# Splitting queries, keys and values ahead of attention and computing all gates in pairs, in a one-core hybrid encoder layer

## The chip, the core and the metric

The kernel is one program on one core of a Trainium2 chip. A core has a matrix engine (PE, with its weight loads shown apart as PEld), a vector engine (DVE), an activation engine (ACT), a general engine (POOL) and a queue engine that issues transfers (SP). They run side by side and wait for each other through semaphores. On-chip memory is SBUF (128 partitions); matmul results land in PSUM, which has eight banks here; DRAM is off the chip, reached by DMA. The metric is the device time of one execution in microseconds, as the median of several runs.

## What is computed

One encoder layer over 1024 tokens of width 1024, in float32. Cut to what matters for the change:

```python
proj = x @ w_in                       # q_a, k_a, v_a, f_a | q_b, f_b, i_b, g_b | gate_a, gate_b
y_a = fox_attention(q_a, k_a, v_a, log_sigmoid(f_a + b_f))   # 8 heads of 64, causal softmax
                                      # logit[t,s] = q_t.k_s/8 + F[t] - F[s]
y_b = hgrn2_chunkwise(silu(q_b), 1 - f, i_b, log(f))         # 4 heads of 128, gated recurrence
merged = sigmoid(gate_a) * (y_a @ w_pa) + sigmoid(gate_b) * (y_b @ w_pb)
x = layer_norm(ALPHA * x + merged @ w_o)
x = layer_norm(ALPHA * x + (silu(g) * u) @ w_ff_out)         # u, g = x @ w_ff_in
```

`gate_a` and `gate_b` are each 1024 columns wide: 16 blocks of 128 columns together, called gates 0 to 15 below.

## The kernel before

**Precision.** Every float32 operand of a big product is split into a high and a low part (`split`: ACT casts the high part, DVE subtracts it from the source), and a product is three matmuls (`mm3`): high by high, high by low, low by high. Each is 128 x 128 weights against 512 columns.

**Strassen pairs.** Many products are done as 2 x 2 block products with 7 sub-products in place of 8 (names p1 to p7). For two gates as a pair that is 7 x 4 x 3 = 84 matmuls, where two plain gates take 2 x 2 x 8 x 3 = 96. The sums that this needs are made by DVE.

**Stages, in order of time.** The values of both branches (`vx`, `vy`); queries and keys by `qk_strassen`, one call for each of four pairs of heads; attention, eight heads; HGRN, four heads; the rest of the gates; the two branch projections (`pps`); the output projection (`o`); the first and the second half of the feed-forward net (`fa`, `fb`, `fc`; then `p`).

**Attention before.** `qk_first` runs `qk_strassen` for the pairs 1, 2, 3, 0. For pairs 1 to 3, `put` stores the float32 result in DRAM (`qk_d`, 12 stores of 128 KB a pair). For pair 0, `qk_heads` splits it into the operands at once. After each pair of heads `qk_load` fetches the next pair (eight loads of 256 KB into `qkr`) and splits it with eight ACT and eight DVE instructions. A head's operands are `q2` (high and low query stacked on the partitions), `k2` (high key twice) and `kl` (low key twice). They sit in the buffers "qk" (six of them; two `q2` and two `kl` a pair) and "kb" (four; two `k2` a pair). Values are kept on the chip as `va` (buffer "v"), and each head splits its part into `vhl` with one ACT and one DVE instruction. The last four blocks of probabilities of a head are up to 1024 wide and take all four buffers "pf", so the wide blocks of a head wait for those of the head before.

**What fills PE's gaps.** Attention and HGRN are chains across PE, DVE, ACT and POOL. Between their steps PE does work that hangs on nothing there: in attention four plain gates (`gate`, results `gps`; as many as the constant `PLAIN` says), then the even gate of the later pairs (`gate_part`, results `ge`: products p1 and p2 of the pair, 24 matmuls), and the projections of the HGRN heads (`hgrn_project`, results `bps`, 144 matmuls a head). Gates 4 to 7 are two pairs interleaved (`pairs`), and gates 8 to 15 four more pairs in a loop, five products (60 matmuls) each after their `gate_part`; both write `gs`.

**Order of the work.** The body of the kernel does not issue instructions. It records them in a `Plan`; `schedule` then places them in time by a table of costs, engine by engine, with the buffers' waiting lines, and `improve` repeats this with ranks counted back from the end (`latest`), `ROUNDS` times, with random slack from the seventh on, and keeps the order whose planned end is earliest. `issue` emits that order; each engine then runs its own list strictly in order. So any edit can change the whole order. All instructions are issued at line 381, which is why all profile rows carry L381. `plan.behind` makes the calls recorded while it is set wait for a given earlier call.

Of the kernel before, what the change touches and what calls it, by code (L numbers as in the profile page):

```python
# [24 lines left out]
FF = 2816  # L25
CHUNKS = [[(0, n)] if n <= NB else [(0, n - w), (n - w, w)] for n, w in
          ((128, 0), (256, 0), (384, 0), (512, 0), (640, 256), (768, 256), (896, 384), (1024, 512))]
PLAIN = 4
MERGE = {"g": "s"}
SPREAD = {"s": 2, "pt": 2, "pv": 1, "g": 1, "h": 2}  # L30
LOOSE = ("ps_s", "gt", "ps_h")
EARLY = 3000
AHEAD = 3000
WARM = 7
ROUNDS = 24
MARGIN = 1.06
SLACK = 400.0
SWITCH = 300.0
# [23 lines left out]
class Plan:  # L62
# [288 lines left out]
    def improve(self, slack, wait):  # L351


        self.turn = list(range(len(self.calls)))
        best = self.schedule(slack, wait), self.end, self.times
        vary = np.random.default_rng(1)
        for n in range(ROUNDS):
            last, self.rank = self.turn, self.latest(slack if n < 6 else slack * vary.uniform(0, 3))
            self.turn = self.rank
            try:  # L360
                order = self.schedule(slack, wait)
            except RuntimeError:
                self.turn = last
                order = self.schedule(slack, wait)
            if self.end < best[1]:
                best = order, self.end, self.times
        order, self.end, self.times = best
        return order
# [16 lines left out]
def trunk(ctx: ExitStack, tc, a: dict, out: bass.AP):  # L385
# [43 lines left out]
    def hs(i):  # L429
        return slice(i * NB, (i + 1) * NB)  # L430
# [283 lines left out]

    ya_d = dram.tile([4, 2, 2, DH, S], F32, name="ya_d")

    def qk_tiles(p):
        return ([full("qk", f"q2_{p}_{i}", F32R) for i in range(2)], [full("kb", f"k2_{p}_{i}", F32R) for i in range(2)],
                [full("qk", f"kl_{p}_{i}", F32R) for i in range(2)])

    def qk_heads(b, hf, o, q2, k2, kl):
        for i in range(2):
            me, ot = slice(i * DH, (i + 1) * DH), slice((1 - i) * DH, (2 - i) * DH)
            if b == 0:
                act.activation(q2[i][me, hs(hf)], o[me], AF.Copy, scale=-0.125)
                dve.scalar_tensor_tensor(q2[i][ot, hs(hf)], o[me], -0.125, f(q2[i])[me, hs(hf)],
                                         op0=ALU.mult, op1=ALU.subtract)
            else:
                act.copy(k2[i][me, hs(hf)], o[me])
                act.copy(k2[i][ot, hs(hf)], o[me])  # L730
                dve.tensor_sub(kl[i][me, hs(hf)], o[me], f(k2[i])[me, hs(hf)])
                act.copy(kl[i][ot, hs(hf)], f(kl[i])[me, hs(hf)])

    qk_d = dram.tile([4, 2, 2, 2, DH, S], F32, name="qk_d")
    for n, x in enumerate((xh, xl)):
        sync.dma_start(s1_d[:, n], f(x[0][:, :, hs(1)]))
    lanes = [0]

    def qk_strassen(p, wtags, btags, tiles=None):

        g, u = (take(t, [KC, P], f"w{n}{p}_r") for t, n in zip(wtags, "qk"))
        for b, t in enumerate((g, u)):
            sync.dma_start(t, a["w_qk"][b, p])
        b11, b12, b21, b22 = g[:, :4], u[:, :4], g[:, 4:], u[:, 4:]
        p1, p5 = (half("ph", f"qk{p}_{i}") for i in ("p1", "p5"))
        oa, ob, oc = (bank(t, f"qk{p}_{t}") for t in btags)

        def mul(n, src, o, first):
            lane = lanes[0]
            lanes[0] ^= 1  # L750
            T = [take(f"w{x}{lane}", [4, P], f"Tqk{p}{n}{x}", F32R) for x in "hl"]
            split(*T, src)
            more = {} if first else {"skip_group_check": True}
            for c in range(4):
                mm3(o, T[0][:, c], T[1][:, c], vops[n][0][c], vops[n][1][c], first and c == 0, c == 3, more)

        def put(b, hf, o):
            if tiles:
                return qk_heads(b, hf, o, *tiles())
            if o is oa:  # L760
                t = half("gt", f"qk{p}_o")
                act.copy(t, o)
                o = t
            for i in range(2):
                for j in range(2):
                    sync.dma_start(qk_d[p, b, i, j, :, hs(hf)], o[i * DH:(i + 1) * DH])

        mul("p1", b11, oa, True)
        act.copy(p1, oa)
        dve.tensor_sub(b12, b12, b11)  # L770
        mul("p5", b12, oc, True)
        if tiles:
            split4(A21, a21)
        t2 = take("tt", [4, P], f"wqk{p}_t2")
        dve.tensor_sub(t2, b22, b12)
        mul("p2", b21, ob, True)
        dve.tensor_add(p1, ob, p1)
        put(0, 0, p1)
        mul("p6", t2, oa, False)
        u2 = half("tt", f"qk{p}_u2")  # L780
        act.copy(u2, oa)
        dve.tensor_sub(b11, t2, b11)
        mul("p7", b11, oa, False)
        act.copy(p5, oa)
        dve.tensor_add(p5, oc, p5)
        put(1, 1, p5)
        mul("p3", b22, oc, False)
        dve.tensor_add(u2, oc, u2)
        put(1, 0, u2)
        dve.tensor_sub(b21, b21, t2)  # L790
        mul("p4", b21, oa, False)
        put(0, 1, oa)

    def qk_load(p):
        q2, k2, kl = qk_tiles(p)
        for b in range(2):
            for hf in range(2):
                for i in range(2):
                    ot = slice((1 - i) * DH, (2 - i) * DH)
                    raw = half(f"w{'hl'[i]}0", f"qkr{p}_{b}{hf}{i}")  # L800
                    sync.dma_start(raw, qk_d[p, b, i, :, :, hs(hf)].rearrange("j d t -> (j d) t"))
                    if b == 0:
                        act.activation(q2[i][:, hs(hf)], raw, AF.Copy, scale=-0.125)
                        dve.scalar_tensor_tensor(q2[i][ot, hs(hf)], raw[ot], -0.125, f(q2[i])[ot, hs(hf)],
                                                 op0=ALU.mult, op1=ALU.subtract)
                    else:
                        act.copy(k2[i][:, hs(hf)], raw)
                        dve.tensor_sub(kl[i][:, hs(hf)], raw, f(k2[i])[:, hs(hf)])
        return q2, k2, kl

    def qk_first():
        made = []

        def tiles():
            if not made:
                made.extend(qk_tiles(0))
            return made

        for p, w, b in ((1, "hl", 0), (2, "kb", 1), (3, "hl", 0), (0, "kb", 1)):
            qk_strassen(p, (w, w), (("s", "pt", "s"), ("h", "pv", "h"))[b], None if p else tiles)  # L820
        return made

    def attention(p, qk):
        q2, k2, kl = qk
        for i in range(2):
            h = 2 * p + i

            r = 2 - 2 * (h % 2)
            nfx = box1[:, r:r + 2, :].rearrange("p a (b t) -> p (a b) t", t=P)
# [1 line left out]
            sync.dma_start(box1[:, r + 1, :], a["causal"])  # L831
            pool.dma_start(box1[:, r + 1, :], nf_d[h].partition_broadcast(P), accum_op=ALU.add)
            vhl = take("hl", [NT, 2, DH], f"vhl{h}", F32R)
            vsrc = va[:, :, h * DH:(h + 1) * DH]
            split(vhl[:, :, 0, :], vhl[:, :, 1, :], vsrc)
            pr = []
            for qb in range(NT):
                n = (qb + 1) * P
                if qb % 4 == 0:
                    sums = small([P, 8], "sums", 3, "ss")  # L840
                sm, rs = sums[:, qb % 4:qb % 4 + 1], sums[:, 4 + qb % 4:5 + qb % 4]
                pt = full("pf", f"p{h}_{qb}") if qb > 3 else half("ph", f"p{h}_{qb}")
                mn = small([P, 3], "soft")
                nm = 3e38
                seen = 0
                for ci, (c0, w) in enumerate(CHUNKS[qb]):
                    sc = bank("s", f"s{h}_{qb}_{ci}")
                    mm(sc[:, :w], q2[i][:, blk(qb)], k2[i][:, c0:c0 + w], start=True, stop=False)
                    mm(sc[:, :w], q2[i][:, blk(qb)], kl[i][:, c0:c0 + w], start=False, stop=True)
                    tail = min(w, 2 * P) if c0 + w == n else 0  # L850
                    for o, m in ((0, w - tail), (w - tail, tail)):
                        if not m:
# [66 lines left out]
    def hgrn_project(h):  # L919
        q, fk, sg = (full("qk", f"hb{n}{h}") for n in "qfg")  # L920
        for bi, dst in ((1, fk), (0, q), (2, sg)):
            plan.early = AHEAD
            w = weights(a["w_b"][bi, h], [KC, P], f"wb{bi}_{h}", 0)
            plan.early = 0
            for hf in range(2):
                o = bank("g", f"bps{bi}_{h}_{hf}")
                project(o, w, hf)
                d = dst[:, hs(hf)]
                if bi < 2:
                    d = dst.rearrange("p (c j t) -> p j c t", c=2, t=P)[:, 2 * hf:2 * hf + 2]  # L930
# [191 lines left out]
            act.copy(t, o)  # L1122
            sync.dma_start(dst, t)

    qk = qk_first()
    for p in range(4):
        attention(p, qk)
        if p < 3:
            qk = qk_load(p + 1)
        else:  # L1130
            qfg = hgrn_project(0)
    box = take("v", [4, S], "box")
    for h in range(HB):
# [689 lines left out]
```

## Time and profile before

| what | value |
|---|---|
| median of 3 runs | 1435.51 us (1433.79 to 1436.5) |
| profiled execution | 1434.72 us, of which the span from first to last instruction is 1432.9 us |
| granted PE clock in it | 0.998 |
| busy: PE, PEld, DVE, ACT, POOL | 99%, 82%, 77%, 47%, 6% of the span |
| moved by DMA | 208.52 MB, mean 146 GB/s |

A row of the instruction groups reads: line, engine, operation, output<-inputs, shapes, count | busy time in us, mean ns of one | idle time of the engine before them and who ended it. A row of the windows reads: stretch in us, then for each engine busy us and count of instructions, then the granted clock, the share of the 16 DMA engines' time, and GB/s. A matmul's duration includes a pipeline that the next matmul overlaps, so the mean ns of one is longer than the distance from one to the next.

### The profile page before, as it was taken

Reading aid. Unit: us, or ns where it says so; the run is one execution under the profiler, and the core shown is the slowest. Engines: PE = TensorE matmul, PEld = TensorE weight load, DVE = VectorE, ACT = ScalarE, POOL = GpSimd, SP = SyncE. Lnnn points to the kernel's source line nnn. Section 1 sums busy time; section 2 is a strip of 40 time slices with the busy share of each in tenths; the row PEclk is TensorE's granted clock in tenths of the full one; section 3 lists DMA queues with packets and bytes.
Section 4 is the critical chain, followed back from the end, with each engine's and each line's share of the span. In section 5 each row is a group of like instructions: output and inputs, shape, how many; then the busy total and the mean of one; then the engine's idle time right before and its main releaser. Section 6 shows DMA issues by size and latency. Waiting matters only on the chain.

```text
span 1432.9 us, 19015 instructions
## 1 busy us (share of the span) xinstructions
PE 1421.4 (99%) x6746; PEld 1182.0 (82%) x6746; DVE 1101.2 (77%) x1904; ACT 669.3 (47%) x1187; POOL 92.0 (6%) x108
## 2 busy tenths in 40 slices
PE   9999999999999999999999999999999999999997
PEld 7788888888888888888888888888888888888886
DVE  7985698976888899655757997666766776789597
ACT  5523788877777763244511543332333334444330
POOL 0000044330001100000000000000000000000001
PEclk9999999999999999999999999999999999999999
DMA  7446666521111377567500233333333326978632
GB/s 269 168 138 172 169 220 194 160 89 45 49 40 45 124 242 216 175 206 271 170 1 28 76 105 123 101 98 111 110 111 110 103 93 195 329 257 271 216 130 89
DMA packets 87839, 208.52 MB, mean 146 GB/s; under 512 B 10032, under 2 KB 11312, under 8 KB 87744
## 3 DMA queue, kind: packets, MB, share of 16 engines
q1 hardware_dynamic: 86592, 203.12, 43.2%
q0 software_dynamic: 1152, 4.19, 1.7%
q8 instruction: 53, 0.87, 0.2%
q14 instruction: 42, 0.34, 0.1%
HBM read 155.57 MB, written 51.71 MB: 145 GB/s over the span
## 4 chain that ended last, share of the span: by engine, by line
PE 96%; DVE 3%; DMA 1%; ACT 0%; issue 0%; SPq 0%; DVEq 0%; ACTq 0%
PE p L381 15%; PE fb L381 11%; PE bps L381 9%; PE fc L381 8%; PE fa L381 8%; PE gs L381 6%; PE o L381 6%; PE pps L381 6%; PE vx L381 4%; PE gps L381 3%; PE qk_s L381 2%; PE vy L381 2%; PE qk_h L381 2%; PE s L381 2%; PE pv L381 2%; PE pt L381 2%
## 5 line engine op out<-in xcount | busy, mean ns | idle before, releaser
L381 PE MATMUL p<-dp 128*128 128x512 f32 (+1 forms) x957 | 210.0, 382 | 0.0
L381 PEld LDWEIGHTS p<-dp 128*128 128x128 f32 x957 | 175.3, 188 | 34.8
L381 PE MATMUL fc<-xs,Tp 128*128 128x512 f32 x528 | 127.2, 389 | 0.8 <-ACT Tp L381 0.8
L381 PE MATMUL fb<-xs,Tp 128*128 128x512 f32 x528 | 127.2, 389 | 0.0
L381 PEld LDWEIGHTS fc<-xs,Tp 128*128 128x128 f32 x528 | 99.1, 188 | 21.8 <-ACT Tp L381 1.2
L381 PEld LDWEIGHTS fb<-xs,Tp 128*128 128x128 f32 x528 | 99.1, 188 | 20.5
L381 PE MATMUL fa<-x,Tp 128*128 128x512 f32 x480 | 115.6, 389 | 0.0
L381 ACT CAST Tp<-t 128x512 fp32r<-128x512 f32 x88 | 54.1, 620 | 117.8 <-PE fc L381 64.9
L381 DVE TENSOR_TENSOR Tp<-t,Tp 128x512 fp32r<-128x512 f32 x88 | 60.7, 691 | 61.2 <-ACT Tp L381 60.6
L381 PEld LDWEIGHTS fa<-x,Tp 128*128 128x128 f32 x480 | 90.1, 188 | 18.7
L381 PE MATMUL bps<-xh,wb_h 128*128 128x512 f32 x192 | 76.6, 399 | 0.0
L381 PE MATMUL bps<-xh,wb_l 128*128 128x512 f32 x192 | 75.6, 398 | 0.0
L381 PE MATMUL bps<-xl,wb_h 128*128 128x512 f32 x192 | 75.2, 392 | 0.0
L381 POOL TENSOR_TENSOR norm<-norm,few 128x1 f32<-128x1 f32 x16 | 15.4, 962 | 880.9 <-DVE norm L381 880.9
L381 ACT CAST dp<-dap 128x1024 fp32r<-128x1024 f32 (+1 forms) x42 | 41.1, 979 | 60.8 <-PE p L381 36.6
L381 DVE TENSOR_TENSOR dp<-dap,dp 128x1024 fp32r<-128x1024 f32 (+1 forms) x42 | 47.5, 1131 | 24.1 <-ACT dp L381 24.1
L381 DVE TENSOR_TENSOR tl<-pt,th 128x512 fp32r<-128x512 f32 (+1 forms) x96 | 52.1, 552 | 13.9 <-ACT th L381 12.4
L381 POOL TENSOR_SCALAR p<-p,sums 128x128 f32<-128x128 f32 (+3 forms) x64 | 52.6, 853 | 88.2 <-DVE sums L381 61.8
L381 PE MATMUL fb<-x,Tp 128*128 128x512 f32 x240 | 57.6, 389 | 0.0
L381 ACT CAST Tp<-wg_r 128x512 fp32r<-128x512 f32 x40 | 24.9, 622 | 61.9 <-PE fb L381 30.0
L381 ACT ACTIVATE p<-p,soft 128x640 f32<-128x640 f32 (+5 forms) x64 | 49.9, 780 | 6.4 <-DVE soft L381 6.1
L381 PEld LDWEIGHTS fb<-x,Tp 128*128 128x128 f32 x240 | 45.0, 188 | 9.4
(683 smaller groups left out, 3447.5 us busy)
## 6 DMA issues: line engine op xcount, KB each, us to landing
dbp<-in_w_fo SPq DMA_DIRECT2D x45, 512.0 KB, 5.1
dap<-a_d SPq DMA_DIRECT2D x35, 512.0 KB, 4.5
wg_r<-in_w_ff SPq DMA_DIRECT2D x22, 512.0 KB, 4.0
wu_r<-in_w_ff SPq DMA_DIRECT2D x22, 512.0 KB, 3.7
a_d<-ar SPq DMA_DIRECT2D x42, 256.0 KB, 2.7
a_d<-as SPq DMA_DIRECT2D x33, 256.0 KB, 3.1
wg_r<-in_w_g SPq DMA_DIRECT2D x16, 512.0 KB, 4.5
sg<-gate_d SPq DMA_DIRECT2D x32, 256.0 KB, 3.4
```

The costliest lines, as they stand in the source:

```text
L381: getattr(q.engine, method)(*args, **kw)
```

## The change

Five edits go together.

1. Gates: `PLAIN` goes from 4 to 0. No plain gate is left; gates 0 to 3 are the two interleaved pairs, and the loop and `gate_part` take six pairs (gates 4 to 15) where they took four.
2. Queries and keys: all four pairs are split in `put`, scaled by -1/8 for queries, and the high and low parts stored in `qk_d` (eight stores of 256 KB a pair). Each head loads its own `q2`, `k2` and `kl` in three loads of 512 KB, with no arithmetic after. `q2` sits in "qk", `k2` and `kl` in "kb". The loads of head h are held behind a late scoring step of head h - 2. `qk_strassen` runs for the pairs 0, 1, 2, 3 with other weight buffers and banks (`QORDER`).
3. Values: eight splits ahead of attention, stored in `v_d` (eight of 512 KB); each head loads its `vhl` (512 KB).
4. The wide probabilities of odd heads take the buffer "v" (`wide`), which `va` held before, and those of even heads keep "pf".
5. Order: 36 rounds for 24, another random seed, a fallback to the last order that worked, and the first HGRN projection writes to the banks "h".

```diff
-PLAIN = 4
+PLAIN = 0
-ROUNDS = 24
+ROUNDS = 36
+QORDER = ((0, "hl", ("s", "pt", "s")), (1, "kb", ("h", "pv", "h")), (2, "hl", ("s", "pt", "s")), (3, "hl", ("h", "s", "h")))
...
-        vary = np.random.default_rng(1)
+        sound = self.turn, self.rank
+        vary = np.random.default_rng(3)
...
+    v_d = dram.tile([HA, P, NT, 2, DH], F32, name="v_d")
+    for h in range(HA):
+        two = take("qk", [NT, 2, DH], f"v{h}", F32R)
+        split(two[:, :, 0, :], two[:, :, 1, :], va[:, :, h * DH:(h + 1) * DH])
+        sync.dma_start(v_d[h], f(two))
+    qk_d = dram.tile([4, 4, P, S], F32, name="qk_d")
...
         def put(b, hf, o):
-            if tiles:
-                return qk_heads(b, hf, o, *tiles())
-            if o is oa:
-                t = half("gt", f"qk{p}_o")
-                act.copy(t, o)
-                o = t
-            for i in range(2):
-                for j in range(2):
-                    sync.dma_start(qk_d[p, b, i, j, :, hs(hf)], o[i * DH:(i + 1) * DH])
+            hi, lo = (half("gt" if n else "tt", f"qk{p}_{b}{hf}{n}", F32R) for n in range(2))
+            if b == 0:
+                act.activation(hi, o, AF.Copy, scale=-0.125)
+                dve.scalar_tensor_tensor(lo, o, -0.125, f(hi), op0=ALU.mult, op1=ALU.subtract)
+            else:
+                split(hi, lo, o)
+            for n, t in enumerate((hi, lo)):
+                sync.dma_start(qk_d[p, 2 * b + n, :, hs(hf)], f(t))
...
+    def qk_load(h):
+        p, i = divmod(h, 2)
+        me = slice(i * DH, (i + 1) * DH)
+        q2, k2, kl = full("qk", f"q2_{h}", F32R), full("kb", f"k2_{h}", F32R), full("kb", f"kl_{h}", F32R)
+        sync.dma_start(f(q2), qk_d[p, :2, me])
+        for n, t in ((2, k2), (3, kl)):
+            src = qk_d[p, n, me]
+            sync.dma_start(f(t), bass.AP(tensor=src.tensor, offset=src.offset, ap=[[0, 2]] + [list(d) for d in src.ap]))
         return q2, k2, kl
...
+    scored = []
+    def attention(p):
         for i in range(2):
             h = 2 * p + i
+            plan.behind = tuple(scored[:h - 1][-1:]) if h >= 2 else ()
+            q2, k2, kl = qk_load(h)
+            plan.behind = ()
...
-            vsrc = va[:, :, h * DH:(h + 1) * DH]
-            split(vhl[:, :, 0, :], vhl[:, :, 1, :], vsrc)
+            sync.dma_start(f(vhl), v_d[h])
             pr = []
+            if i:
+                wide = take("v", [4, S], f"p{h}_w")
...
-                pt = full("pf", f"p{h}_{qb}") if qb > 3 else half("ph", f"p{h}_{qb}")
+                pt = (wide[:, qb - 4] if i else full("pf", f"p{h}_{qb}")) if qb > 3 else half("ph", f"p{h}_{qb}")
...
+                if qb == NT - 1:
+                    scored.append(len(plan.calls) + 3)
...
-                o = bank("g", f"bps{bi}_{h}_{hf}")
+                o = bank("h" if h < 1 else "g", f"bps{bi}_{h}_{hf}")
...
-    qk = qk_first()
+    qk_all()
     for p in range(4):
-        attention(p, qk)
-        if p < 3:
-            qk = qk_load(p + 1)
-        else:
+        attention(p)
+        if p == 3:
             qfg = hgrn_project(0)
```

More of the change, by code (lines that the diff above doesn't have):

```diff
@@ L355, in improve @@
         best = self.schedule(slack, wait), self.end, self.times
-        vary = np.random.default_rng(1)
+        sound = self.turn, self.rank
+        vary = np.random.default_rng(3)
         for n in range(ROUNDS):
-            last, self.rank = self.turn, self.latest(slack if n < 6 else slack * vary.uniform(0, 3))
+            self.rank = self.latest(slack if n < 6 else slack * vary.uniform(0, 3))
             self.turn = self.rank
@@ L362, in improve @@
             except RuntimeError:
-                self.turn = last
+                self.turn, self.rank = sound
                 order = self.schedule(slack, wait)
+            sound = self.turn, self.rank
             if self.end < best[1]:
@@ L715, in trunk @@
     ya_d = dram.tile([4, 2, 2, DH, S], F32, name="ya_d")
[L717 to L721, printed above, removed]
-        for i in range(2):
[L723 to L727, printed above, removed]
-            else:
[L729 to L734, printed above, removed]
+    v_d = dram.tile([HA, P, NT, 2, DH], F32, name="v_d")
[4 more added lines that the diff above has]
+    qk_d = dram.tile([4, 4, P, S], F32, name="qk_d")
     for n, x in enumerate((xh, xl)):
@@ L737, in trunk, with qk_strassen @@
     lanes = [0]
-    def qk_strassen(p, wtags, btags, tiles=None):
+    def qk_strassen(p, wtags, btags, last=False):
         g, u = (take(t, [KC, P], f"w{n}{p}_r") for t, n in zip(wtags, "qk"))
@@ L757, in put @@
         def put(b, hf, o):
-            if tiles:
-                return qk_heads(b, hf, o, *tiles())
-            if o is oa:
-                t = half("gt", f"qk{p}_o")
-                act.copy(t, o)
-                o = t
-            for i in range(2):
-                for j in range(2):
-                    sync.dma_start(qk_d[p, b, i, j, :, hs(hf)], o[i * DH:(i + 1) * DH])
+            hi, lo = (half("gt" if n else "tt", f"qk{p}_{b}{hf}{n}", F32R) for n in range(2))
[6 more added lines that the diff above has]
+                sync.dma_start(qk_d[p, 2 * b + n, :, hs(hf)], f(t))
         mul("p1", b11, oa, True)
@@ L771, in qk_strassen @@
         mul("p5", b12, oc, True)
-        if tiles:
+        if last:
             split4(A21, a21)
@@ L792, in qk_strassen, with qk_all @@
         put(0, 1, oa)
[L794 to L808, printed above, removed]
-        return q2, k2, kl
[L811 to L824, printed above, removed]
+    def qk_load(h):
[6 more added lines that the diff above has]
+            sync.dma_start(f(t), bass.AP(tensor=src.tensor, offset=src.offset, ap=[[0, 2]] + [list(d) for d in src.ap]))
+        return q2, k2, kl
+    def qk_all():
+        for p, w, b in QORDER:
+            qk_strassen(p, (w, w), b, p == QORDER[-1][0])
+    scored = []
+    def attention(p):
         for i in range(2):
             h = 2 * p + i
+            plan.behind = tuple(scored[:h - 1][-1:]) if h >= 2 else ()
+            q2, k2, kl = qk_load(h)
+            plan.behind = ()
             r = 2 - 2 * (h % 2)
@@ L847, in attention @@
                     sc = bank("s", f"s{h}_{qb}_{ci}")
-                    mm(sc[:, :w], q2[i][:, blk(qb)], k2[i][:, c0:c0 + w], start=True, stop=False)
-                    mm(sc[:, :w], q2[i][:, blk(qb)], kl[i][:, c0:c0 + w], start=False, stop=True)
+                    mm(sc[:, :w], q2[:, blk(qb)], k2[:, c0:c0 + w], start=True, stop=False)
+                    mm(sc[:, :w], q2[:, blk(qb)], kl[:, c0:c0 + w], start=False, stop=True)
                     tail = min(w, 2 * P) if c0 + w == n else 0
@@ L1123, in gate_part @@
             sync.dma_start(dst, t)
-    qk = qk_first()
+    qk_all()
     for p in range(4):
-        attention(p, qk)
-        if p < 3:
-            qk = qk_load(p + 1)
-        else:
+        attention(p)
+        if p == 3:
             qfg = hgrn_project(0)
```

## The prediction

> **What bounds the kernel now.** I read the page first: busy shares, slices, the chain that ended last.
>
> ```profile
> span 1432.9 us, 19015 instructions
> ...
> PE 1421.4 (99%) x6746; PEld 1182.0 (82%) x6746; DVE 1101.2 (77%) x1904; ACT 669.3 (47%) x1187; POOL 92.0 (6%) x108
> ...
> PE 96%; DVE 3%; DMA 1%; ACT 0%; issue 0%; SPq 0%; DVEq 0%; ACTq 0%
> ```
>
> PE is busy in all but 1432.9 - 1421.4 = 11.5 us, and 96% of the chain is PE. Busy can hide waits, because a matmul's row lasts longer than its distance to the next. So I took windows and counted instructions, then the longest pieces of the chain.
>
> ```profile
> 100.00:150.00 50.00, 50.00 (x222) 41.42 (x221) 23.77 (x37) 17.80 (x32) 0.25 (x1) 1.00 0.65 167
> 250.00:300.00 50.00, 49.01 (x284) 41.21 (x284) 45.49 (x145) 41.55 (x96) 19.55 (x22) 1.00 0.52 160
> 550.00:600.00 50.00, 50.00 (x223) 41.39 (x222) 40.57 (x61) 14.36 (x21) 0.00 (x0) 1.00 0.72 221
> 170.00:345.00 175.00, 174.01 (x981) 147.04 (x980) 145.31 (x440) 139.45 (x308) 58.64 (x72) 1.00 0.47 144
> 345.00:520.00 175.00, 174.92 (x966) 150.35 (x965) 154.53 (x244) 131.84 (x247) 13.27 (x12) 1.00 0.26 84
> ```
>
> ```profile
> 265.59 5.73 DMA qkr<-qk_d
> 535.05 73.70 PE gs L381 x325
> ```
>
> In the chain, 325 matmuls of 512 columns run without a break in 73.70 us: 0.2268 us each. Where only such matmuls run (100 to 150, 550 to 600) the count is 222, which is 0.225 us each, so PE is full. Attention (about 170 to 345) and HGRN (345 to 520) mix in short matmuls, yet PE idles there only 0.99 and 0.08 us. Every matmul removed should therefore show in the end time, if the others close up.
>
> The Trainium skill, "Trainium Kernel Development and Optimization", Performance Expectations, warns against exactly my first reading: matmul busy time is a bad metric because matmuls are pipelined, and weight-load busy time is a better one. By that the 82% of PEld would leave 18% to gain. The trace disagrees for this kernel: the unbroken stretches themselves show 41.4 of 50 us, and attention and HGRN 147.04 and 150.35 of 175, 84% and 86%, so 82% over the span is what a full PE looks like here.
>
> **The change, part by part.**
>
> *Gates, PLAIN 4 to 0.* These rows give the counts.
>
> ```profile
> L381 PE MATMUL gps<-xh,wg_h 128*128 128x512 f32 x64 | 26.3, 411 | 0.0
> L381 PE MATMUL gps<-xl,wg_h 128*128 128x512 f32 x64 | 26.2, 410 | 0.0
> L381 PE MATMUL gps<-xh,wg_l 128*128 128x512 f32 x64 | 26.1, 408 | 0.0
> L381 PE MATMUL ge<-xh,we_l 128*128 128x512 f32 x32 | 13.1, 410 | 0.0
> L381 PE MATMUL ge<-xh,we_h 128*128 128x512 f32 x32 | 12.7, 403 | 0.0
> L381 PE MATMUL ge<-xl,we_h 128*128 128x512 f32 x32 | 12.7, 397 | 0.0
> L381 PE MATMUL gs<-gs,Tgp_8h 128*128 128x512 f32 x24 | 7.4, 389 | 0.0
> L381 PE MATMUL gs<-gs,Tgp_8l 128*128 128x512 f32 x12 | 4.7, 389 | 0.0
> L381 PE MATMUL gs<-xh,Tgp_8h 128*128 128x512 f32 x8 | 3.1, 389 | 0.0
> L381 PE MATMUL gs<-xl,Tgp_8h 128*128 128x512 f32 x8 | 3.1, 389 | 0.0
> L381 PE MATMUL gs<-xh,Tgp_8l 128*128 128x512 f32 x8 | 3.1, 389 | 0.0
> ```
>
> The plain gates are 3 x 64 = 192 matmuls. A pair of the loop is 24 + 12 + 8 + 8 + 8 = 60, plus 96 / 4 = 24 in `gate_part`: 84. All gates now: 192 + 2 x 84 + 4 x 84 = 696. After: 8 x 84 = 672. That is 24 fewer, 24 x 0.2268 = 5.44 us of PE. Nothing else changes the number of matmuls.
>
> The mixing has a price of its own: the rows of `gps` last 410 ns on average against 389 in unbroken runs, 192 x 21 ns = 4.0 us. The 48 new `ge` matmuls bring back 48 x 14 ns = 0.7 us, and I expect the first HGRN projection, moved into attention, to be mixed as the plain gates were: 144 x 21 ns = 3.0 us at most. So mixing gains between 0.3 and 3.3 us; I take nothing, because the `bps` now mix in HGRN too.
>
> The filler is what could be missed. Out of the two stretches go 192 x 0.2268 + 4.0 = 47.5 us, in come 48 x 0.2268 = 10.9 us: PE work 348.93 - 47.5 + 10.9 = 312 us. The two added pairs, 120 matmuls or 27.2 us, run after HGRN, where 550 to 600 shows PE full with DVE at 40.57 of 50 and DMA at 0.72. They cost nothing beyond their matmuls.
>
> *Splits.* What leaves attention:
>
> ```profile
> L381 DVE TENSOR_TENSOR kl<-qkr,k 128x512 fp32r<-128x512 f32 x12 | 10.4, 868 | 0.0
> L381 DVE SCALAR_TENSOR_TENSOR q<-qkr,q 64x512 fp32r<-64x512 f32 x12 | 8.7, 722 | 0.2
> L381 DVE TENSOR_TENSOR vhl<-va,vhl 128x512 fp32r<-128x512 f32 x8 | 6.8, 848 | 0.8 <-ACT vhl L381 0.7
> L381 DVE TENSOR_TENSOR wg_l<-wg_r,wg_h 128x512 fp32r<-128x512 f32 x8 | 6.0, 756 | 0.6 <-ACT wg_h L381 0.6
> L381 ACT CAST k<-qkr 128x512 fp32r<-128x512 f32 x12 | 7.5, 623 | 4.1 <-DMA qkr<-qk_d 4.0
> ```
>
> DVE loses 10.4 + 8.7 + 6.8 + 6.0 = 31.9 us in the two stretches and gains four `ge` weight splits, 4 x 0.756 = 3.0: it goes from 145.31 + 154.53 = 299.8 to 270.9 us. Against 312 us of PE that is 87%, as 299.8 against 348.9 was 86%. The densest DVE row above is 45.49 of 50 us, 91%; at that rate 270.9 us need 298 us, 14 less than PE has. So over both stretches PE stays the bound, with a thin reserve.
>
> What arrives ahead of attention: 8 value splits and 16 splits in `put`, less 8 of `qk_heads`: DVE +16 x 0.72 = 11.5 us, beside PE work in which DVE is busy 23.77 of 50 us, so it has room. These instructions also use PSUM banks and the "gt" buffers a little longer; I cost that at nothing, and at 0.7 us for each of 16 if PE had to wait for a bank, 11 us at worst. The near row is PE at 50.00 of 50 in that stretch, so nothing.
>
> *Transfers.*
>
> ```profile
> DMA packets 6228, 13.72 MB, mean 161 GB/s; under 512 B 1040, under 2 KB 1104, under 8 KB 6224
> ...
> qk_d<-qk_p SPq DMA_DIRECT2D x24, 128.0 KB, 3.2
> ...
> DMA packets 10140, 25.23 MB, mean 144 GB/s; under 512 B 1136, under 2 KB 1136, under 8 KB 10122
> ...
> qkr<-qk_d SPq DMA_DIRECT2D x20, 256.0 KB, 4.6
> ...
> 1200.00:1250.00 50.00, 50.00 (x222) 41.39 (x222) 36.48 (x39) 23.39 (x28) 0.00 (x0) 1.00 0.89 312
> ```
>
> The two totals are the stretches 85 to 170 and 170 to 345. Into the first go 8 x 0.52 MB of values, and 32 stores of 0.262 MB in place of 48 of 0.131: 13.72 + 4.2 + 2.1 = 20 MB in 85 us, 235 GB/s. In attention each head now loads four tiles of 0.52 MB, 16.8 MB in all, in place of 24 x 0.262 = 6.3: 25.23 + 10.5 = 35.7 MB in 175 us, 204 GB/s. With four fewer weight blocks it is a little less. The last row carries 312 GB/s with PE full, so both fit on average.
>
> A tile now travels through DRAM before use: 3.2 us for the store and 4.6 for the load, about 8 us. Queries, keys and values are stored during the Strassen stage, pair 0 first, with three calls of 84 matmuls, 57 us, behind it, so the first head's tiles have landed in time. Later heads load while the head before runs, some (345 - 170) / 8 = 22 us, for which "kb" has room: four buffers, two a head. The hold behind the scoring of head h - 2 makes SP wait; behind it stand the stores of `ya` and `ge`, whose "gt" buffers ACT then waits for, and the loads of the gate weights. A late load costs what one cost before:
>
> ```profile
> PE pv L381 <- ACT th L381: 0.8, 1, 0.8
> ```
>
> The piece "DMA qkr<-qk_d" at 265.59 above is that case: ACT stood at `k<-qkr` for the load (4.0 us in all in its row), `th` queued behind it, PE lost 0.8 us here and 0.99 in the window. After the change no ACT or DVE instruction splits loaded keys, so this goes: -1.0. In its place PE itself can stand for a load, once a head at most for seven heads, from 0 to 7 x 1.0 us. I take 1.0, since one such wait of three pair loads came to the surface before. The two cancel.
>
> The Trainium skill, "DMA: Bandwidth & Descriptors", Anatomy of one DMA, speaks against this edit: every DMA pays about 2 us of fixed time, most of it the receipt, heaviest where DRAM is the target; with its fit a 0.52 MB tile takes 3.2 us. An estimate from that page is 6.4 us for out and back, near the 7.8 us of the rows; if every head paid it, the sum would be the third rival's or worse.
>
> *The overlap of two heads and the new order.* Odd heads' wide blocks no longer wait for "pf". This shortens a chain behind PE's filler, so I cost it at nothing, and at nothing again if the planned order doesn't use it, because the sum rests on PE's matmuls.
>
> *Sum*, against the profiled execution: 1434.72 - 5.44 - 1.0 + 1.0 = 1429.3 us. The median of the runs stands 0.79 above that execution, so the forecast is 1430.1, a gain of 5.4 us or 0.38%. A change below 0.2%, 2.9 us, can't be told from none.
>
> **The rivals.**
>
> *More than the matmuls.* If also the mixing price and the waits in attention go: 5.44 + 3.3 + 1.07 = 9.8 us, 1425.7. For it: DVE and ACT have less to do between scores. Against: the fillers still alternate with short matmuls. It holds if `bps` fall to 389 ns.
>
> *Each head waits for its loads.* Seven heads lose 0.99 us more than I took, 6 x 0.99 = 5.9 us: 1436.0, no change. For it: 204 GB/s comes in bursts, and three loads of a head wait for the same scoring step. Against: 22 us of a head for tiles that land in about 5.
>
> *HGRN runs short of filler (the other side).* Before, part of the `ge` ran in its last third:
>
> ```profile
> 450.00:500.00 50.00, 4.73 (x17) 3.24 (x18) 0.59 (x1) 1.00 0.28 91
> 500.00:550.00 50.00, 12.01 (x44) 7.68 (x42) 2.34 (x4) 1.00 0.72 230
> ```
>
> These are 61 matmuls, 61 x 0.2268 = 13.8 us. If attention, which has lost its 192, takes all `ge` for itself, HGRN has its DVE chain of 154.53 us alone, 170 us at 91%, and PE has 174.92 - 13.8 = 161 us to put beside it. PE then stands 9 us at the least, and the whole 13.8 if the following pairs can't start for lack of banks: 1430.1 + 13.8 = 1443.9, slower. It decides from 24 matmuls on, where the idle time passes 5.4 us. For it: the reserve of 14 us is for both stretches together. Against: attention lost 31.9 us of DVE work and so needs less filler, and the first projection is free to move into it.
>
> *The change doesn't do what it says*: the order that comes out keeps the heads apart. The time is then the forecast's, for the reason given with that edit.
>
> **How the numbers follow.** Forecast 0.60, more 0.10, loads 0.13, HGRN 0.17. The first two are faster: 0.70. The loads are no change, 0.13; HGRN is slower, 0.17. The likeliest case alone spans 1427 to 1432.5: 3 us less if all mixing goes, 2.4 more if some loads wait. The range takes in "more" down to 1425 and "loads" up to 1437, and leaves out HGRN, 0.17.
>
> **What would show it.** `gps` gone, `ge` at 144, six pairs of `gs` rows, 6722 matmuls in place of 6746. PE at 50.00 in the windows of attention and HGRN, and the unbroken row of `gs` longer by some 27 us. DVE down to about 271 us in attention and HGRN together, which should end 37 us sooner (312 for 349). Loads at fault would be PE waiting on `q` or `k` DMAs; HGRN at fault would be PE idle behind DVE between `lp` rows. The forecast is wrong if PE's idle time over the span passes 11.5 us by more than 2.5.

## The result, and the profile after

| kernel | median | runs | ratio, 95% interval |
|---|---|---|---|
| before | 1434.65 us (lowest 1433.43) | | |
| after | 1627.42 us (1626.44 to 1628.63) | 4 | 1.1343, 1.1323 to 1.1362 |

The change makes the kernel 13% slower; the forecast was 1430.1 us. A ratio is estimated from all the runs, so it can differ a little from the quotient of two medians. The profiled execution took 1627.74 us. From its page come the span, the busy row, the granted clock in 40 slices of 40.6 us, and the chain by engine:

```profile
span 1625.9 us, 18939 instructions
...
PE 1451.3 (89%) x6722; PEld 1201.9 (74%) x6722; DVE 1105.4 (68%) x1912; ACT 652.3 (40%) x1160; POOL 91.6 (6%) x108
...
PEclk9997877768779999999999999999999999999999
...
PE 68%; issue 6%; DMA 3%; DVE 3%; SPq 1%; POOL 1%; ACT 1%; DVEq 0%; POOLq 0%; ACTq 0%
```

The 24 matmuls are gone as forecast (6722). But PE now stands 1625.9 - 1451.3 = 174.6 us, where it stood 11.5: +163.1 us. And its busy time grew by 29.9 us although it has less to do: 163.1 + 29.9 = 193.0 us, the whole growth of the span. The clock row says where: the slices of about 120 to 490 us, which are the end of the query and key stage and nearly all of attention (its last `pv` matmuls start at 514 us, the first `lp` of HGRN at 519).

The windows show the same by stage (columns: stretch, then busy us and count of PE, PEld, DVE, ACT, POOL, then granted clock, DMA share, GB/s):

```profile
100.00:150.00 50.00, 39.09 (x173) 31.94 (x171) 21.36 (x34) 15.44 (x29) 0.00 (x0) 0.91 0.42 139
250.00:300.00 50.00, 27.66 (x123) 23.11 (x123) 21.88 (x86) 24.16 (x50) 5.89 (x8) 0.70 0.27 92
550.00:600.00 50.00, 50.00 (x282) 43.10 (x281) 44.19 (x73) 38.62 (x75) 5.58 (x5) 1.00 0.20 64
170.00:345.00 175.00, 85.54 (x391) 70.01 (x390) 58.97 (x184) 58.63 (x123) 23.10 (x28) 0.73 0.42 132
345.00:520.00 175.00, 115.73 (x590) 96.05 (x591) 93.66 (x263) 88.13 (x190) 36.86 (x47) 0.79 0.32 96
...
288.00:301.00 13.00, 5.36 (x19) 4.54 (x20) 1.47 (x3) 4.62 (x6) 0.00 (x0) 0.50 0.33 101
441.00:450.00 9.00, 6.26 (x37) 5.15 (x36) 7.26 (x25) 5.89 (x13) 0.00 (x0) 0.96 0.13 52
```

Before, attention ran from 170 to 345 with PE at 174.01 of 175. Now that stretch has 391 matmuls in place of 981, no engine is full, and neither are the DMAs. From 288 to 301 PE is busy 5.36 of 13 us and the clock is granted at 0.50: standing PE is also slowed PE: a `bps` matmul lasts 628 ns there, where those of before last 392 to 399 on average. With 24 matmuls fewer, this is where the +29.9 us can come from. (The Trainium skill, "TensorE: Matmul & The Clock Gate", Part 1, states that a window with an idle PE halves the clock; the row agrees.) From 550 on, in HGRN, PE is full.

The odd number is in the last row: DMA share 0.13 at 52 GB/s. The stretch 440 to 460 in the DMA view, in 40 slices of 0.5 us (busy tenths, then GB/s):

```profile
DMA  1111111111111111111111679999889999989821
GB/s 74 49 57 49 49 57 49 57 49 49 57 49 49 57 49 49 57 49 57 49 49 49 123 213 344 360 164 197 287 229 303 197 270 266 266 311 373 328 94 66
```

For 11 us the rate stands flat near 52 GB/s, then jumps to over 200 within a microsecond. What SP does beside it, in the timeline (start, us, what):

```profile
418.70 8.44 SPq L384 DMA_DIRECT2D k<-qk_d  x1
427.23 3.98 SPq L384 DMA_DIRECT2D kl<-qk_d  x1
431.31 19.41 SPq L384 DMA_DIRECT2D box<-in_causal  x1
450.77 1.06 SPq L384 DMA_DIRECT2D box<-nf_d  x1
451.92 1.75 SPq L384 DMA_DIRECT2D vhl<-v_d  x1
```

The two key loads go out, and the next transfer's issue lasts 19.41 us; two loads of 0.524 MB at 52 GB/s are 1.049 MB / 52 GB/s = 20.2 us. PE shows such loads landing one after the other. In the stretch from 288 to 301 its scoring matmuls wait first for `k`, then for `kl` of the same head (start, us, what, idle time before it and who ended it):

```profile
289.18 0.66 PE L384 MATMUL s<-k,q 128*128 128x384 f32 x1 [11.28 <-DMA k<-qk_d]
...
299.39 0.79 PE L384 MATMUL s<-kl,q 128*128 128x384 f32 x2 [6.46 <-DMA kl<-qk_d]
```

The second key comes 10.2 us after the first. A DMA share of 0.13 is 2 of 16 engines. And the loads that the change adds have an outermost index of size 2: `qk_d[p, :2, me]` (copy, row, column) for queries, `ap=[[0, 2], ...]` (twice the same rows) for keys. That is theory A: these loads run on two of the 16 DMA engines (called narrow below, all others wide), 0.524 MB / 52 GB/s = 10.1 us each, 24 of them, and SP, which issues in order, holds all that stands behind. Which engines carry a load the trace doesn't show; two is read from the share and the rate. The Trainium skill states the rule: "DMA: Bandwidth & Descriptors", section "Why a DMA increments its semaphore by 16 and not by 1", lets a DMA use as many engines as the largest number up to 16 that divides both patterns' slowest dimensions, and its "Rules for kernel authors" warn of just such a leading zero-stride copy.

The waits of the whole span give who suffers (us in total, times, longest):

```profile
POOL box L384 <- DMA box<-in_causal: 185.6, 6, 33.9
...
PE s L384 <- DMA kl<-qk_d: 41.0, 5, 10.4
...
PE pt L384 <- DVE tl L384: 35.5, 3, 32.9
...
PE s L384 <- DMA k<-qk_d: 34.5, 5, 11.3
...
DVE tl L384 <- DMA qk_d<-qk: 33.5, 1, 33.5
```

Only 75.5 us is PE standing for keys themselves. The largest wait for a DMA is POOL's for `box`, the bias load, which is a wide transfer that stands behind them.

### The profile page after: what moved, and what is told of

Read it like the earlier page. It is cut to its first block, busy times and chain, and to the rows that moved or that the text cites. A ratio compares the mean times of both kernels' runs of the same rounds, so it can differ in the third digit from the quotient of the medians.

```text
span 1625.9 us, 18939 instructions
## 1 busy us (share of the span) xinstructions
PE 1451.3 (89%) x6722; PEld 1201.9 (74%) x6722; DVE 1105.4 (68%) x1912; ACT 652.3 (40%) x1160; POOL 91.6 (6%) x108
## 4 chain that ended last, share of the span: by engine, by line
PE 68%; issue 6%; DMA 3%; DVE 3%; SPq 1%; POOL 1%; ACT 1%; DVEq 0%; POOLq 0%; ACTq 0%
PE p L384 13%; PE fb L384 10%; PE gs L384 7%; PE fc L384 7%; PE fa L384 7%; PE bps L384 6%; PE o L384 5%; PE pps L384 5%; PE ge L384 2%; DMA ya_d<-ya 2%; PE lp L384 1%; DMA qk_d<-qk 1%; SPq L384 1%; PE op L384 1%; PE pt L384 1%
## 5 line engine op out<-in xcount | busy, mean ns | idle before, releaser
L384 PE MATMUL s<-k,q 128*128 128x512 f32 (+3 forms) x96 | 39.2, 412 | 71.9 <-DMA k<-qk_d 34.5
L384 ACT CAST th<-pt 128x512 fp32r<-128x512 f32 (+1 forms) x96 | 45.5, 479 | 86.2 <-PE pt L384 79.9
L384 PE MATMUL bps<-xh,wb_h 128*128 128x512 f32 x192 | 79.9, 417 | 0.0
L384 PEld LDWEIGHTS s<-k,q 128*128 128x128 f32 x96 | 22.0, 230 | 78.3 <-issue 31.3
L384 PE MATMUL bps<-xl,wb_h 128*128 128x512 f32 x192 | 79.1, 413 | 0.0
L384 PE MATMUL s<-kl,q 128*128 128x512 f32 (+3 forms) x96 | 38.1, 405 | 41.0 <-DMA kl<-qk_d 41.0
L384 PE MATMUL pt<-ident,p 128*128 128x128 f32 x184 | 33.6, 284 | 33.4 <-DVE tl L384 33.4
```

The lines of the kernel that those rows point to most:

```text
L384: getattr(q.engine, method)(*args, **kw)
```

## The experiments

Theories besides A: **B**, the way through DRAM itself is too slow; **C**, without the plain gates PE has no filler; later **D**, the values' trip and the stores pile up at the start of attention, and **E**, chance of the planned order. Each edit that adds or removes instructions changes the whole planned order, so differences of a few us between such kernels carry that too.

### One index moved outward

After, with the same bytes and loads, rows outermost:

```diff
-        sync.dma_start(f(q2), qk_d[p, :2, me])
+        sync.dma_start(f(q2), qk_d[p, :2, me].rearrange("n d t -> d n t"))
...
-            sync.dma_start(f(t), bass.AP(tensor=src.tensor, offset=src.offset, ap=[[0, 2]] + [list(d) for d in src.ap]))
+            d0, t0 = (list(d) for d in src.ap)
+            sync.dma_start(f(t), bass.AP(tensor=src.tensor, offset=src.offset, ap=[d0, [0, 2], t0]))
```

> The changed kernel with the three loads of a head written with the row as outer index (row, copy, column) in place of (copy, row, column); same bytes, same count of transfers, same planned order; partitions of q2, k2 and kl are permuted alike. Theory A (a load whose outer index has size 2 runs on 2 of the 16 DMA engines, at 49 to 57 GB/s in the changed kernel's trace, and all later transfers queue behind it): the loads take some 4 to 6 us, the granted clock is back at 1.00, and the time falls from 1627 to 1425 to 1440 us. Theory B (the trip through DRAM itself is too long, or the heads wait for their stores): nothing changes, over 1600. Theory C (the planned order is bad because the plain gates are gone and PE lacks filler): nothing changes, over 1600; if A and C both hold, between 1450 and 1600.

Measured 1436.89 us against 1435.81, ratio 1.0011 (1.0002 to 1.0021): 190.5 us less than after, with the same instructions. Its page, windows, and the DMA issues of 170 to 345 (size of one, median us to landing):

```profile
span 1434.9 us, 18939 instructions
...
PE 1418.4 (99%) x6722; PEld 1179.3 (82%) x6722; DVE 1103.9 (77%) x1912; ACT 650.7 (45%) x1160; POOL 93.1 (6%) x108
```

```profile
100.00:150.00 50.00, 50.00 (x223) 41.41 (x222) 30.59 (x51) 22.25 (x42) 0.00 (x0) 1.00 0.69 225
150.00:200.00 50.00, 47.19 (x247) 39.37 (x246) 39.95 (x119) 35.88 (x75) 15.50 (x18) 1.00 0.92 314
200.00:250.00 50.00, 47.33 (x270) 40.58 (x270) 37.39 (x132) 40.59 (x89) 15.84 (x22) 0.97 0.80 259
```

```profile
q<-qk_d SPq DMA_DIRECT2D x6, 512.0 KB, 5.2
...
k<-qk_d SPq DMA_DIRECT2D x5, 512.0 KB, 4.4
kl<-qk_d SPq DMA_DIRECT2D x5, 512.0 KB, 5.6
...
qk_d<-qk SPq DMA_DIRECT2D x5, 256.0 KB, 9.8
v_d<-v SPq DMA_DIRECT2D x2, 512.0 KB, 13.8
```

The loads land in 4.4 to 5.6 us. Of the 191.0 us between the two spans, 158.1 are PE's idle time (174.6 to 16.5) and 32.9 its busy time (1451.3 to 1418.4). So A is the cause of the 13%; B and C together can only hold what is left, the 6.8 us between this kernel and the forecast.

### How much each load costs

After, with chosen loads issued as two transfers of 64 rows, each with its rows outermost. In one kernel `k2` and `kl` (so one narrow load a head is left), in the other `q2` (two are left). `plan.two` holds the numbers of the calls:

```diff
+                if i in self.two:
+                    src = args[1]
+                    for j in range(2):
+                        part = bass.AP(tensor=src.tensor, offset=src.offset + j * src.ap[0][0], ap=[list(d) for d in src.ap[1:]])
+                        getattr(q.engine, method)(args[0][j * DH:(j + 1) * DH], part)
+                    continue
```

> The changed kernel with k2 and kl each loaded as two transfers of 64 rows, and q2 as it was (outer index of size 2). Theory A: one narrow load of about 10 us a head is left, beside some 20 us that a head of attention takes, so most of the loss goes: 1430 to 1470 us. Theories B and C: over 1600.

> The changed kernel with q2 loaded as two transfers of 64 rows, and k2 and kl as they were. Theory A: two narrow loads a head, about 20 us, which is as long as a head of attention: between the other two, 1480 to 1570 us, with PE still waiting for k and kl. Theories B and C: over 1600.

Measured 1502.2 us (ratio 1.0462, 1.0439 to 1.0485) and 1570.71 (1.0939, 1.0918 to 1.096): both above what was expected, the first by 32 us. With 0, 8, 16 and 24 narrow loads the medians are 1436.89, 1502.2, 1570.71 and 1627.42: +65, +69 and +57 us per eight, some 8 us for each load of 10. So even one narrow load a head isn't hidden by the head before, although 10 us are less than a head's 22. The reason shows in what is not narrow. In the DMA issues of the kernel with one narrow load a head, against the kernel with none:

```profile
box<-in_causal SPq DMA_DIRECT2D x8, 512.0 KB, 10.3
...
k<-qk_d SPq DMA_DIRECT2D x16, 256.0 KB, 20.8
...
vhl<-v_d SPq DMA_DIRECT2D x8, 512.0 KB, 17.7
```

```profile
box<-in_causal SPq DMA_DIRECT2D x8, 512.0 KB, 6.4
...
vhl<-v_d SPq DMA_DIRECT2D x8, 512.0 KB, 4.8
```

The value tiles, wide in both, land after 17.7 us where they took 4.8 (in the first kernel that is the one landing that could be matched), and the halves of the keys, 64 rows each and wide too, take 20.8. So a narrow load costs what it delays, and not what it carries.

### The same fault put into the kernel before

First only the outer index of size 2 for `qkr`, then the same with one spare row after each 64, so that the two halves are no longer one piece of DRAM:

```diff
-                    sync.dma_start(raw, qk_d[p, b, i, :, :, hs(hf)].rearrange("j d t -> (j d) t"))
+                    sync.dma_start(raw, qk_d[p, b, i, :, :, hs(hf)])
```

```diff
-    qk_d = dram.tile([4, 2, 2, 2, DH, S], F32, name="qk_d")
+    qk_d = dram.tile([4, 2, 2, 2, DH + 1, S], F32, name="qk_d")
...
-                    sync.dma_start(qk_d[p, b, i, j, :, hs(hf)], o[i * DH:(i + 1) * DH])
+                    sync.dma_start(qk_d[p, b, i, j, :DH, hs(hf)], o[i * DH:(i + 1) * DH])
...
-                    sync.dma_start(raw, qk_d[p, b, i, :, :, hs(hf)].rearrange("j d t -> (j d) t"))
+                    sync.dma_start(raw, qk_d[p, b, i, :, :DH, hs(hf)])
```

> The kernel before, with the 24 loads of 256 KB into qkr given with an outer index of size 2 (head half, row, column) in place of 128 rows; nothing else. Theory A: each load takes about 5 us on two engines, eight of them 40 us a pair, as long as a pair of heads takes, and ACT stands behind them: slower than before by 15 to 120 us. Theories B and C: the same as before, within 3 us.

> The kernel before with qk_d padded by one row after each 64, so that the two head halves of a qkr load can't be merged into 128 rows and its outer index has size 2; 24 loads of 256 KB. Theory A: each takes some 5 us on two engines and holds up what is queued behind it; by the loss of 57 to 69 us for eight loads of 512 KB in the three kernels so far, 24 of half the size cost 60 to 110 us: 1495 to 1545 us. Without it: as before, within 3 us, as e4_before_two, whose two halves lie one behind the other in DRAM.

The first: 1436.33 us, ratio 1.0006 (0.9996 to 1.0017), no change, against 15 to 120 us expected. The second: 1515.81, ratio 1.0555 (1.0531 to 1.0578), inside its expectation. A window of the second, while its loads run:

```profile
192.00:199.00 7.00, 3.98 (x16) 3.36 (x17) 2.45 (x7) 3.01 (x8) 0.91 (x1) 0.55 0.13 49
```

The same share and rate as after, without the change's splits, values or gates: A is shown in the other kernel too. In the first kernel the halves lie back to back with one stride, and the fault doesn't appear. That they were merged into 128 rows is the likely reason: the gap alone brings the fault back, and SP's time to issue one load (ns: least, median, most) has the median of before, 320, in the first kernel and not in the second:

```profile
L381 SPq DMA_DIRECT2D qkr<-qk_d x24: 319/320/640, 157.9 to 269.6; - x24
```

```profile
L381 SPq DMA_DIRECT2D qkr<-qk_d x24: 487/499/5789, 157.6 to 335.8; - x24
```

### The gates

`PLAIN` 0 in the kernel before, and `PLAIN` 4 in the kernel with rows outermost (all else of the change in):

```diff
-PLAIN = 4
+PLAIN = 0
```

```diff
-PLAIN = 0
+PLAIN = 4
```

> The kernel before with PLAIN 0 for 4 and nothing else: 24 matmuls fewer, the splits and loads of before. Theory F (the floor of the prediction: 24 x 0.2268 = 5.4 us, PE closes up): 1428 to 1432 us. Theory C (attention, with its splits still in it, lacks filler): 1436 us or more, with PE idle in attention or HGRN.

> e1_rows_first with PLAIN 4 for 0: all edits of the change but the gates, loads on 16 engines. Theory D (what eats the gain in e1_rows_first is the pile-up of stores and loads between 150 and 250 us, whatever the filler): 24 matmuls more on top of the same stalls, 1440 to 1444 us. Theory C (it is the missing filler): the stalls go, and the time is that of before or a little less, 1432 to 1437 us.

The first: 1455.39 us against 1434.68, ratio 1.0132 (1.0117 to 1.0148). Its windows:

```profile
200.00:250.00 50.00, 41.91 (x230) 31.44 (x230) 43.16 (x131) 39.02 (x92) 21.12 (x24) 0.98 0.68 204
250.00:300.00 50.00, 44.69 (x252) 32.91 (x251) 45.93 (x154) 41.94 (x100) 21.99 (x26) 0.98 0.42 122
```

The attention of before, with its splits, starves PE without the plain gates, as far as one order shows it; PE's longest waits are for DVE's `tl` (4.4 us) and ACT's `th` (3.4 us) and `ya` (3.2 us). C holds there. The second: 1436.34, ratio 1.0007 (0.9996 to 1.0017), the same as without plain gates. With splits and loads in place the 24 matmuls bring nothing net. In one window for each, 150 to 350, the one with plain gates, then the one without:

```profile
150.00:350.00 200.00, 196.69 (x1120) 168.15 (x1119) 167.68 (x478) 161.13 (x332) 57.22 (x75) 1.00 0.60 197
```

```profile
150.00:350.00 200.00, 193.44 (x1100) 164.22 (x1099) 170.16 (x485) 153.32 (x333) 62.54 (x76) 0.99 0.61 199
```

PE stands 3.3 us in the first and 6.6 in the second: 3.3 of the 5.4 us go there.

A third try, with two plain gates left, fitted neither theory:

> e1_rows_first with PLAIN 2: 12 matmuls fewer than before, two plain gates left as filler. Theory C: the filler needed in attention is mostly there, and half the gain shows, 1431 to 1434 us. Theory D: as e1_rows_first and e6_spread_plain4, 1435 to 1438 us.

1440.08 us, ratio 1.0029 (1.0017 to 1.0042), slower than both neighbours. Its PE stood 4.55 us in 150 to 200 alone, 4.2 of them at once, while DVE waited 5.2 us for a late bias load (`box<-nf_d`). That is a transfer of the burst, as in theory D; why it comes later in this order than in its neighbours is open.

### Where the last 6.8 us went

The kernel with rows outermost, with values kept on the chip and split by each head as before; "v" is then taken, so all wide probabilities go back to "pf". Then the same with the values through DRAM as in the change (only the last two pieces of the diff), to part the two:

```diff
-    v_d = dram.tile([HA, P, NT, 2, DH], F32, name="v_d")
-    for h in range(HA):
-        two = take("qk", [NT, 2, DH], f"v{h}", F32R)
-        split(two[:, :, 0, :], two[:, :, 1, :], va[:, :, h * DH:(h + 1) * DH])
-        sync.dma_start(v_d[h], f(two))
...
-            sync.dma_start(f(vhl), v_d[h])
+            vsrc = va[:, :, h * DH:(h + 1) * DH]
+            split(vhl[:, :, 0, :], vhl[:, :, 1, :], vsrc)
...
-            if i:
-                wide = take("v", [4, S], f"p{h}_w")
...
-                pt = (wide[:, qb - 4] if i else full("pf", f"p{h}_{qb}")) if qb > 3 else half("ph", f"p{h}_{qb}")
+                pt = full("pf", f"p{h}_{qb}") if qb > 3 else half("ph", f"p{h}_{qb}")
```

> e1_rows_first with the values kept on the chip and split in each head as before, and the wide probabilities of all heads in pf again: 8.4 MB of transfers fewer around 90 to 250 us, no overlap of two heads' wide blocks. Theory D (the gain of 5.4 us is eaten by the pile-up of stores and loads between 150 and 250 us): the transfer rate in 150 to 200 falls from 314 towards 250 GB/s, the idle time there shrinks, and the time is 1430 to 1435 us. Theory C (attention without plain gates lacks PE work to put beside its chain, which the overlap of heads shortens): PE stands more, 1440 to 1456 us.

> e1_rows_first with the wide probabilities of all heads in pf again, values through DRAM as in the change: it parts the two edits that e9_values_kept undid together. Theory D (the transfers of the values cost the gain): as e1_rows_first, 1435 to 1439 us. If the overlap of two heads was the harm, it falls with e9_values_kept, 1430 to 1433 us; if the overlap helps, it is slower than e1_rows_first, 1439 us or more.

Values kept: 1431.36 us against 1435.9, ratio 0.9973 (0.9957 to 0.9989), a little faster than before, and inside D's range; in 150 to 200 the rate fell from 314 to 282 GB/s, and PE's idle time from 2.81 to 0.80 us. Values through DRAM without the overlap: 1444.66, ratio 1.0065 (1.0052 to 1.0079), outside D's range and in the one named for an overlap that helps. With the kernel that has both (1436.89), these two orders put the overlap at 1444.66 - 1436.89 = 7.8 us of gain and the values' trip at 1444.66 - 1431.36 = 13.3 us of loss; the change pays the one to get the other.

These are single orders, and the second has a stall that need not come from the missing overlap. In 150 to 200 its PE stands 5.63 us, 5.0 of them at once, right behind a late bias load:

```profile
DVE p L384 <- DMA box<-nf_d: 6.6, 1, 6.6
```

The kernels with two plain gates and with another seed (below) have the overlap, and their PE stands 4.55 us in that stretch too, with such waits of 5.2 and 4.9 us. How much of the 7.8 us is the overlap itself therefore stays open. The rate alone doesn't decide either: with four plain gates PE stood only 1.56 us there, at 323 GB/s.

Values kept, in the same window as above:

```profile
150.00:350.00 200.00, 198.33 (x1125) 168.28 (x1124) 170.44 (x477) 165.35 (x343) 62.39 (x75) 1.00 0.57 179
```

PE stands 1.67 us in place of 6.6. Two waits of 150 to 345 say what was pushed back, first with the values through DRAM, then with them kept:

```profile
DVE tl L384 <- DMA qk_d<-qk: 7.5, 2, 4.3
```

```profile
DVE tl L384 <- DMA qk_d<-qk: 1.8, 1, 1.8
```

`tl` takes a buffer "tt", which a store of queries or keys still reads (`hi` in `put` sits there); the stores land in 9.8 us in that burst (the issues above). That is D, as far as a few orders can show it: it is a late transfer of the burst each time, a store here and a bias load in the other three.

> e1_rows_first with the random seed of before (1 for 3): same instructions, another planned order. Theory E (a difference of a few us is the luck of the order found): it moves by 2 to 10 us either way from 1436.9. If it stays within 2 us, the order found isn't what decides.

Another seed for the order: 1437.85 us, ratio 1.0017 (1.0006 to 1.0029), 1 us from the kernel with rows outermost. One more order doesn't find the gain, which speaks against E but doesn't exclude it.

### Dearer transfers in the plan

The plan prices a transfer by its bytes alone, so it could not know of narrow ones. With rows outermost, and every transfer made dearer:

```diff
-    LAT = {"PE": 197.0, "ACT": 131.0, "DVE": 128.0, "POOL": 66.0, "SP": 2500.0}
-    OWN = {"PE": 0.0, "ACT": 0.0, "DVE": 127.0, "POOL": 60.0, "SP": 2500.0}
+    LAT = {"PE": 197.0, "ACT": 131.0, "DVE": 128.0, "POOL": 66.0, "SP": 4000.0}
+    OWN = {"PE": 0.0, "ACT": 0.0, "DVE": 127.0, "POOL": 60.0, "SP": 4000.0}
...
-        return float(o.nbytes()) / 300.0
+        return float(o.nbytes()) / 220.0
```

> e1_rows_first with the plan's price of a transfer raised: 220 bytes a ns for 300, and 4.0 us to landing for 2.5, near the 4.8 to 5.7 us that its trace shows. Same instructions, another order. Theory D: the order leaves the late transfers more time, the waits of DVE for the stores of qk_d (7.5 us) shrink, and the time is 1429 to 1434 us. If it stays at 1436 to 1440, the pile-up can't be planned away this way.

1478.17 us, ratio 1.0292 (1.0273 to 1.0311): a miss. PE is busy only 42.93 of the first 50 us, long before attention, and stands 7.10 us in 200 to 250. A plan that holds every transfer to be slow is worse; whether a better price would plan the pile-up away stays open.

## Why the prediction failed

**The step that failed is *Transfers*.** It priced the loads of `q2`, `k2` and `kl` by the rows of `qkr<-qk_d` (4.6 us) and `qk_d<-qk_p` (3.2 us), which are plain blocks of rows, and by bytes ("both fit on average"). It never asked how an access pattern with a 2 outermost is spread over the engines. The loads took 10 us, and 24 of them, with what stood behind, cost 190 us where the step had 1.0, and 7.0 at worst. The row that could have warned was not in the trace of before, which had no load of this shape; the shape itself was in the diff. The fit taken from the Trainium skill ("DMA: Bandwidth & Descriptors", Anatomy of one DMA) is stated there for DMAs issued from GpSimd; SP issues these loads, and its 3.2 us stand against 10 here.

**"A late load costs what one cost before"** failed with it. 1.0 us was one ACT wait behind which little stood. In the change SP's in-order queue stands behind each load, and through it the biases, values and stores. The rival *each head waits for its loads* named the right mechanism and gave it 0.99 us a head; the runs gave about 8 us a load, 24 us a head. Its argument against, 22 us of a head for tiles that land in 5, turns round with 10 us tiles: three are 30 us.

**Gates**: right in count, 6722. Unbroken, 24 matmuls are 5.4 us; with values kept PE's busy time is 1417.8, 3.6 below before, and the median 4.5.

**PE as the bound**: right only where loads keep up. The 193.0 us lie in waits, and the clock of a waiting PE.

**HGRN short of filler**: it did not come. HGRN's window (550 to 600 after) has PE at 50.00, and with rows outermost PE is at 175.00 of 175 from 345 to 520. Filler was short, but in attention: the kernel before without plain gates lost 20.7 us there. The claim that attention, freed of 31.9 us of DVE work, needs less filler is borne out for queries and keys: the kernel with values kept has neither plain gates nor the overlap, splits its values in attention as before, and takes 1431.36 us against those 1455.39. The two also differ in the search for the order and in some buffers and banks.

**More than the matmuls**: this rival's sign, `bps` at 389 ns, did not come; with rows outermost they last 400 to 404 ns, where those of before last 392 to 399.

**Splits ahead of attention**: right at nothing; with rows outermost PE is at 50.00 of 50 from 100 to 150.

**"204 GB/s, both fit on average"**: even with wide loads it failed by a few us. The average over attention was near (193 GB/s with rows outermost, 170 to 345), but its first part ran at 314 GB/s with a share of 0.92, and where the 128 KB stores of before landed in 3.2 us, the five of 256 KB issued after 170 took 9.8 (over all 32 the median is 4.4).

**The overlap at nothing**: perhaps mis-sized; one pair of orders gives 7.8 us of gain as long as the values go through DRAM, and part of that may be the late bias load.

**What would show it** named PE waiting on `q` or `k` DMAs, and an idle time of PE over 14 us; both came, at 75.5 us of such waits for keys and 174.6 us.

## What to carry to other kernels

Before pricing a new transfer by its bytes, read its access pattern: here an outermost dimension of 2 held a load to a DMA share of 0.13 and 10 us, and rows outermost brought it back to 4.4 to 5.6. So put rows outermost and copies inside. A narrow load is paid by everything behind it in its queue, so look at the flat rate and share in the DMA view and not only at who waits for that tile. And when a new DRAM trip buys an on-chip buffer, price both sides: here, by one order each, the trip cost 13.3 us and taking the overlap away 7.8, part of which may have another cause.

## What the runs showed of the hardware

- Loads whose outermost index has size 2 moved at 52 GB/s (512 KB each) and 49 GB/s (256 KB each) with a DMA share of 0.13, and two of 512 KB came 10.2 us apart; the same 512 KB with rows outermost landed in 4.4 to 5.6 us.
- An outer 2 over halves that lie back to back in DRAM cost nothing (ratio 1.0006); with a gap of one row between them it cost 5.55%.
- Behind narrow loads the issue of one DMA on SP lasted 19.41 us, where that of the same bias load took 0.34 to 0.73 us between wide ones.
- A high rate alone does not stop PE. From 150 to 200 us PE lost 2.81 us at 314 GB/s behind a late store, 4.55 at 277 behind a late bias load, and 1.56 at 323 (rows outermost, with none, two and four plain gates); the kernel before carried 312 GB/s with PE full at 1200 to 1250, in the feed-forward net.
